# First loads in small pieces on one queue, low parts ahead of squares, and a memory sum placed later in a decoder step's projections

## The chip, the cores and the metric

The kernel runs on one core of a Trainium2 chip. The metric is device microseconds of one execution; the kernel before took 626.89 us (median of 3 runs, 626.23 to 627.23).

## The reference, cut to what matters

One layer of a hybrid decoder is computed for 256 prompt tokens and 32 decode tokens (8 sequences of 4), 288 tokens in all, with model width 2048:

```
mkv  = rms_norm(mem_prompt, mem_norm_g) @ w_mem_kv          # 256 memory tokens -> 8 tiles of 128 columns (4 K, 4 V)
h    = rms_norm(x, norm_g)
z    = h @ w_in                                             # 52 tiles of 128 columns: q, memory q, K/V, convolution, gates
...                                                         # gated convolution, sparse attention, memory attention
y    = x + concat(groups * gates) @ w_out                   # 16 tiles of 128 columns
out  = rms_norm(y, final_g)
```

Two norms matter here: the memory's, whose sum of squares over 2048 entries gives one factor per memory token (`rstd_m`), and x's (`rstd_x`). The outputs are the normed result, all new K and V rows, the memory's K and V, and the updated window and convolution buffers.

## The kernel before, in words

**Layout.** Everything is held transposed: the width of 2048 lies as 16 chunks (k = 0 to 15) of 128 partitions, the tokens lie along the free axis. A weight tile of 128 output columns is 16 blocks of 128x128, loaded as two halves of 128x1024 (512 KB each). Halves are numbered in the order of use, s = 0, 1, 2, ...: s 0 to 15 are the memory's 8 tiles, from s = 16 on come the 52 tiles of the input projection, then the output projection.

**Products.** Halves 0 to 3 (the memory's tiles 0 and 1, `first_tiles`, L267) are multiplied in plain fp32 against the scaled memory; TensorE runs such a matmul as two instructions, so that they are 64. Their order is tile 0, tile 1 for chunks 0 to 7, then tile 0, tile 1 for chunks 8 to 15. From s = 4 on a product is split: a weight's high part (`w_hi`, L221, a rounding copy on ScalarE) and its low part (`w_lo`, L226, raw minus high on VectorE) meet the high and low parts of the activation in three matmuls for each of the half's 8 chunks, 24 in all (`product_half`, L243). In half s ScalarE's copy for half s+2 and VectorE's subtraction for half s+1 are issued first; from half 6 on the low weights are used by the last 8 of the 24 matmuls. Raw halves have 5 buffers, high parts 3, low parts 2. The load of half s+5 or s+6 is issued inside half s, when its buffer's reader has been issued (`w_load`, L214), and it goes on GpSimd's queue from half 5 on, on SyncE's below.

**The order of the work** is written out by hand. `chunk()` (L158) counts a step about every 12 matmuls and lets every running generator issue its next few instructions. A generator's `yield n` means "again n steps later", and `until(VEC)` (L143) means "when a planner's clock for TensorE has passed its clock for VectorE". Every engine then works through its instructions in this order; nothing is reordered on the chip. The step numbers of the start: half 0 ends at step 2, half 1 at 4, half 2 (with tile 0 handed on) at 6, half 3 at 8, half 4 at 10, half 5 at 12, half 6 at 14, half 7 at 16.

**Memory.** 16 chunks of 256 tokens come in pieces (`m_load`, L756); the norm's weights lie in front of chunk 0. `m_scale` (L804) multiplies four chunks by the norm's weights on VectorE, rounds them to the high part on ScalarE and squares the raw values on ScalarE, in place. After halves 1 and 3 VectorE subtracts the low parts (L285). `mem_rstd` (L838) runs from step 7: three additions of 128x1024 on VectorE, two folds, then four tiny matmuls (`ssq`) that sum over partitions, placed at step 10; the factor is computed and spread over partitions by four more matmuls at step 14. Tiles 0 and 1 leave PSUM unscaled and are scaled in SBUF afterwards; tiles 2 to 7 are multiplied by the factor straight out of PSUM (`mem_tile`, L976).

**x.** Its tokens come once as rows (five loads, `xn_load`, L816) for the squares that ScalarE sums at steps 7 to 11 (`sum_x`, L910), and once transposed (`x_load`, L762; four loads of 3, 9, 3 and 1 chunks). `x_load` of the first three chunks is issued in half 2, the others behind the memory's factor (L879), into buffers that hold the memory's raw chunks before. At step 16 x's factor is spread by TensorE, and from step 18 on `prep_x` (L890) scales, rounds and subtracts, three chunks at a time. Its last act, one step after its last subtraction, is `branch_gates` (L945): 32 narrow matmuls of scaled x.

**Around it.** From step 19 on six buffers are filled with cache pages on SyncE's queue (`load_next`, L711), whose products run beside the projections from s = 16 on. Before the first data, WARM = 5 matmuls of zeros keep TensorE busy (L792).

Of the kernel before, what the change touches and what calls it, by code (L numbers as in the profile page):

```python
# [19 lines left out]
KT = 16  # L20
# [43 lines left out]
XSQ_AT = (7, 8, 9, 10, 11)  # L64
X_AT = (16, 17)
KV_ORDER = (2, 4, 3, 5, 0, 1)
# [3 lines left out]
WARM = 5  # L70
# [6 lines left out]
def decode_step(ctx, tc, xT, xN, xD, memT, cst, w_in, w_mem, w_out, w_bg, pt, ptv, ckc, ckk, ckv, wk, wv, mk, mv,  # L77
# [136 lines left out]
    def w_load(s):  # L214
        if s < NH:
            raws[s] = pw.tile([128, 1024], F32, name=f"w{s}", tag="wr", bufs=WR)
            if s > 1:
                (nc.gpsimd if s >= WR else nc.sync).dma_start(raws[s], wsrc[s])  # L218
            loading(DMA_PIECE)
# [23 lines left out]
    def product_half(out, hi, lo, first, last):  # L243
# [10 lines left out]
        for n, (_, a, b) in enumerate(mm):  # L254
            if s == DIRECT and n == 0:
                w_load(s + WR)
            if n == LOAD_AT:
                w_load(s + WR + 1)
            matmul(out, a, b, start=(first and n == 0), stop=(last and n == 23))
# [7 lines left out]
    def first_tiles():  # L267
# [3 lines left out]
        for k0 in (0, 8):  # L271
            for i in range(2):
# [472 lines left out]
    for i in range(3):  # L745
        t = pbig.tile([128, CS if i == 0 else 1024], F32, name=f"mraw{i}", tag="S" if i == 0 else "big", bufs=1 if i == 0 else 3)
        o = KT if i == 0 else 0
        if i == 0:
            mng = t[:, 0:KT]
            m_first = t[:, 0:KT + 512]  # L750
# [5 lines left out]
    def m_load(k, eng=nc.sync):  # L756
        if k == 0:
            eng.dma_start(m_first, memT[:, 0:KT + 512])
        else:
            eng.dma_start(m_raw[k // 4][:, k % 4:k % 4 + 2, :], memT[:, KT + k * 256:KT + (k + 2) * 256].rearrange("p (k n) -> p k n", n=256))  # L760

    def x_load(k0, n):  # L762
# [4 lines left out]
        nc.sync.dma_start(raw[:, :n * NT].rearrange("p (c n) -> p c n", n=NT), xT[:, k0:k0 + n, :])  # L767
        xr.extend(raw[:, j * NT:(j + 1) * NT] for j in range(n))
        xg.extend((k0 + j, raw[:, j * NT:min(j + 3, n) * NT]) for j in range(0, n, 3))
# [31 lines left out]
    macc = m_raw[0].rearrange("p k n -> p (k n)")  # L801
    m_flat = lambda k: m_raw[k // 4].rearrange("p k n -> p (k n)")

    def m_scale(k):  # L804
# [3 lines left out]
        act.activation(m_flat(k), m_flat(k), AF.Square)  # L808

    m_scale(0)  # L810
    m_scale(4)
# [14 lines left out]
    def first_loads(s):  # L826
        if s == 0:
            xn_load(4)
            xn_load(0)
# [759 lines left out]
```

## Time and profile before

| | |
|---|---|
| median of 3 runs | 626.89 us |
| profiled execution | 623.95 us |
| its span, first to last instruction | 621.6 us |
| mean granted TensorE clock | 0.989 |
| HBM read and written | 182.31 MB and 13.60 MB |

How to read it: PE is TensorE's matmuls, PEld its weight loads, DVE is VectorE, ACT ScalarE, POOL GpSimd, SP SyncE. A row of the timeline gives start, length, engine, line, operation, output<-input, shape and count, and in brackets the idle time before it and what ended it. Line L117 is the helper through which all matmuls go, L134 the one for VectorE and ScalarE, so that groups are told apart by their tiles: `zf` is the product of halves 0 to 3, `z` of all others, `mraw` the memory's raw chunks and their squares, `m` its high and low parts, `w`, `wh`, `wl` the weights and their parts, `st` the six buffers (x's rows at first), `rx` x's chunks, `x` its parts, `ssq` the memory's sum and its spread, `Vc` its spread factor, `mixed` (at the start) the scaled memory and the memory's K tiles.

### The profile page before, as it was taken

The page shows a single profiled execution, that of the slowest core. Times are in us where ns is not written, and L with a number is a line of the kernel's source. Part 1 is how long each engine was busy: PE and PEld are TensorE (multiplying, and loading weights), DVE is VectorE, ACT ScalarE, POOL GpSimd, SP SyncE. Part 2 cuts the span into 40 slices and gives each one's busy share as a digit, 9 for nine tenths or more (in the row PEclk, how much of TensorE's full clock was granted, in tenths as well). Part 3 has the DMA queues.
Part 4 walks back from the last instruction along what each step waited for, and adds up shares of the span by engine and source line. Part 5 has one row for each costly group of instructions (what it writes and reads, how often), then busy time and mean ns, then how long its engine had stood idle before and what let it go on. Part 6 is the DMA issues. An engine that isn't in the chain of part 4 may idle for free.

```text
span 621.6 us, 13341 instructions
## 1 busy us (share of the span) xinstructions
PE 605.4 (97%) x4897; PEld 561.1 (90%) x4897; DVE 458.4 (74%) x737; ACT 285.4 (46%) x498; POOL 210.4 (34%) x291
## 2 busy tenths in 40 slices
PE   8899999999999999999999999999999999999993
PEld 6799999989999999988988988988889889999993
DVE  4759899979586689978876879969586533457764
ACT  4736545453555435325334443444534444446560
POOL 2212654535144333324555432323113444122200
PEclk9899999999999999999999999999999999999997
DMA  8999699989989998988888799898979988478723
GB/s 310 396 389 355 218 316 309 354 287 361 330 264 346 390 403 302 372 283 298 285 324 266 243 377 297 307 338 289 388 261 331 331 322 314 143 242 304 234 91 152
DMA packets 74353, 188.40 MB, mean 303 GB/s; under 512 B 8688, under 2 KB 25488, under 8 KB 73904
## 3 DMA queue, kind: packets, MB, share of 16 engines
q0 software_dynamic: 27344, 105.20, 48.0%
q1 hardware_dynamic: 45792, 79.86, 36.2%
q10 hardware_dynamic: 1152, 2.50, 1.2%
q8 instruction: 38, 0.62, 0.4%
q14 instruction: 27, 0.22, 0.1%
HBM read 182.31 MB, written 13.60 MB: 315 GB/s over the span
## 4 chain that ended last, share of the span: by engine, by line
PE 87%; DVE 7%; DMA 2%; issue 2%; ACT 1%; ACTq 0%; DVEq 0%; SPq 0%
PE z L117 70%; PE od L117 3%; PE sk L117 3%; PE acc L117 2%; PE s L117 2%; DVE pooled L134 2%; DMA mraw<-memT 1%; DVE wl L134 1%; PE pt L122 1%; PE pv L122 1%; DVE ysum L134 1%; DVE mraw L134 1%; DMA st<-ckk 1%; DVE st L134 1%; PE smd L117 1%
## 5 line engine op out<-in xcount | busy, mean ns | idle before, releaser
L117 PE MATMUL z<-x,wh 128*128 128x288 f32 x1664 | 255.2, 302 | 0.4 <-ACT wh L134 0.4
L134 DVE TENSOR_TENSOR wl<-w,wh 128x1024 fp32r<-128x1024 f32 x148 | 184.5, 1247 | 81.9 <-PE z L117 47.6
L117 PEld LDWEIGHTS z<-x,wh 128*128 128x128 f32 x1664 | 230.0, 188 | 9.4 <-issue 7.3
L134 ACT ACTIVATE wh<-w 128x1024 fp32r<-128x1024 f32 x148 | 155.0, 1052 | 21.1 <-PE z L117 19.8
L117 PE MATMUL z<-x,wl 128*128 128x288 f32 x832 | 127.1, 295 | 0.1
L117 PEld LDWEIGHTS z<-x,wl 128*128 128x128 f32 x832 | 115.7, 188 | 0.4 <-DVE wl L134 0.4
L344 POOL TENSOR_TENSOR st<-st,cst 128x512 f32<-128x512 f32 x56 | 64.8, 1160 | 115.9 <-issue 57.7
L218 POOL DMA_DIRECT2D w<-w_in x104 | 58.1, 559 | 92.4 <-DVE wl L134 70.9
L134 DVE TENSOR_REDUCE pooled<-st 128x16 f32<-128x1024 f32 x56 | 67.8, 1211 | 10.3 <-POOL st L344 10.3
L134 DVE TENSOR_TENSOR st<-st,cst 128x512 f32<-128x512 f32 x56 | 40.0, 716 | 2.7 <-DMA st<-ckc 2.6
L566 POOL DMA_INDIRECT st<-ckv,rows_v x29 | 30.9, 1066 | 29.1 <-PE od L117 13.9
L218 POOL DMA_DIRECT2D w<-w_out x32 | 17.5, 550 | 59.3 <-DVE wl L134 41.9
L117 PE MATMUL z<-y,wh 128*128 128x288 f32 x256 | 37.0, 297 | 0.0
L117 PE MATMUL z<-y1a,wh 128*128 128x288 f32 x224 | 35.2, 298 | 0.0
L117 PEld LDWEIGHTS z<-y,wh 128*128 128x128 f32 x256 | 35.1, 188 | 0.0
L117 PEld LDWEIGHTS z<-y1a,wh 128*128 128x128 f32 x224 | 31.5, 188 | 1.6 <-issue 0.8
L117 PE MATMUL z<-m,wh 128*128 128x256 f32 x192 | 29.1, 299 | 0.0
L117 PEld LDWEIGHTS z<-m,wh 128*128 128x128 f32 x192 | 26.4, 202 | 0.6 <-issue 0.5
L134 ACT ACTIVATE P<-P,nm 128x128 f32<-128x128 f32 (+1 forms) x32 | 14.2, 444 | 26.7 <-DVE nm L134 26.7
L134 ACT ACTIVATE ysum<-z 128x288 f32<-128x288 f32 x16 | 6.6, 412 | 34.0 <-PE z L117 34.0
L134 ACT ACTIVATE se<-z 128x288 f32<-128x288 f32 x16 | 6.5, 408 | 28.6 <-PE z L117 28.6
L117 PE MATMUL z<-y,wl 128*128 128x288 f32 x128 | 19.6, 296 | 0.0
(283 smaller groups left out, 719.6 us busy)
## 6 DMA issues: line engine op xcount, KB each, us to landing
w<-w_in POOLq DMA_DIRECT2D x104, 512.0 KB, 6.2
st<-ckc SPq DMA_DIRECT2D x112, 256.0 KB, 5.6
w<-w_out POOLq DMA_DIRECT2D x32, 512.0 KB, 4.9
st<-ckk SPq DMA_DIRECT2D x112, 128.0 KB, 4.7
w<-w_mem POOLq DMA_DIRECT2D x11, 512.0 KB, 8.1
o_wk<-wk POOLq DMA_DIRECT2D x8, 512.0 KB, 6.1
o_wv<-wv POOLq DMA_DIRECT2D x8, 512.0 KB, 6.5
qk<-ckc SPq DMA_DIRECT2D x16, 256.0 KB, 6.2
```

The costliest lines, as they stand in the source:

```text
L117: nc.tensor.matmul(out, a, b, **kw)
L122: nc.tensor.transpose(out, a, b)
L134: return getattr(self.engine, name)(*args, **kw)
L218: (nc.gpsimd if s >= WR else nc.sync).dma_start(raws[s], wsrc[s])
L344: done.append(eng.tensor_tensor(tm[:, :, kv], tm[:, :, kv], acmp[:, kv].unsqueeze(1).unsqueeze(1).to_broadcast([128, 2, 4, 64]), op=ALU.mu ...
L566: nc.gpsimd.indirect_dma_start(t, None, ckv, bass.IndirectOffsetOnAxis(ap=rows_v[:, j * 4 + b:j * 4 + b + 1], axis=0))
```

## The change

- **First loads.** Chunk 0 of the memory and chunk 1 come as loads of their own, half 0 comes in pieces of 256, 256 and 512 columns. Half 1 moves from ScalarE's queue to SyncE's. Halves 5 to 13 move from GpSimd's queue to SyncE's (ON_SYNC = 14).
- **x.** Its row pieces are issued one or two with each of halves 0 to 3, behind that half's weight load, and squared at steps 7, 8, 10, 12, 13. Its transposed chunks come in six loads of at most three chunks, one in half 3 and one in each half after it.
- **Memory.** The squares no longer stand in `m_scale`. In half 1 all low parts are issued, and then the first addition, weight 4's high part, and only then the squares of chunks 8 to 15. The running sum has a buffer of its own (`buffers[5]`). `mem_rstd` starts one step later, does two additions and the folds, and places the four `ssq` matmuls at step 13 and the spread at step 17.
- **Tiles 2 and 3** leave PSUM unscaled, as tiles 0 and 1, and are scaled in SBUF.
- WARM is 3 instead of 5, and `branch_gates` starts with `until(VEC)`.

```diff
-XSQ_AT = (7, 8, 9, 10, 11)
+XSQ_AT = (7, 8, 10, 12, 13)
+ON_SYNC = 14
-WARM = 5
+WARM = 3
...
-                (nc.gpsimd if s >= WR else nc.sync).dma_start(raws[s], wsrc[s])
+                (nc.gpsimd if s >= ON_SYNC else nc.sync).dma_start(raws[s], wsrc[s])
...
             if n == LOAD_AT:
                 w_load(s + WR + 1)
+                next(x_next, None)
...
-                        if i == 1:
-                            for k in (k0, k0 + 4):
-                                vec.tensor_tensor(m_hl[1][:, k:k + 4, :], m_g(k, 4), m_hl[0][:, k:k + 4, :].bitcast(F32),
-                                                        op=ALU.subtract)
-                            if k0 == 0:
-                                for k in (8, 12):
-                                    m_scale(k)
+                        if s == 1:
+                            for k in (0, 4):
+                                m_low(k)
+                            for k in (8, 12):
+                                m_scale(k)
+                            for k in (8, 12):
+                                m_low(k)
+                            m_add(4)
+                            w_hi(4)
+                            for k in (8, 12):
+                                m_square(k)
...
+            nc.sync.dma_start(t.rearrange("p (c n) -> p c n", n=NT), xT[:, k0 + j:k0 + j + m, :])
...
+            yield
+    def x_loads():
+        for k0, n in ((0, 3), (3, 9), (12, 3), (15, 1)):
+            yield from x_load(k0, n)
...
-    m_load(0, nc.scalar)
-    nc.sync.dma_start(raws[0][:, :512], wsrc[0][:, :512])
-    m_load(2, nc.scalar)
+    nc.scalar.dma_start(m_first, memT[:, 0:KT + 256])
+    nc.sync.dma_start(raws[0][:, :256], wsrc[0][:, :256])
+    m_load(1, 1, nc.scalar)
+    nc.sync.dma_start(raws[0][:, 256:512], wsrc[0][:, 256:512])
+    m_load(2, 2, nc.scalar)
     nc.sync.dma_start(raws[0][:, 512:], wsrc[0][:, 512:])
-    m_load(4, nc.scalar)
+    m_load(4, 2, nc.scalar)
     m_load(6)
-    nc.scalar.dma_start(raws[1], wsrc[1])
+    nc.sync.dma_start(raws[1], wsrc[1])
...
-    macc = m_raw[0].rearrange("p k n -> p (k n)")
+    macc = buffers[5]
...
+    def m_square(k):
+        act.activation(m_flat(k) if k else macc, m_flat(k), AF.Square)
...
     def mem_rstd():
-        for k in (4, 8, 12):
-            vec.tensor_tensor(macc, macc, m_flat(k), op=ALU.add)
-            yield 1
+        m_add(8)
+        yield 1
+        m_add(12)
+        yield 1
         for n in (512, 256):
             vec.tensor_tensor(macc[:, :n], macc[:, :n], macc[:, n:2 * n], op=ALU.add)
+        yield 3
...
-            if i < 2:
+            if i < 4:
                 vec.tensor_tensor(dst, dst, rstd_m, op=ALU.mult)
...
-        for s, l in ((3, 9), (12, 3), (15, 1)):
-            x_load(s, l)
...
     def branch_gates():
-        yield 1
+        yield from until(VEC)
...
-        if i < 2:
+        if i < 4:
             act.activation(dst, z, AF.Copy)
...
-    spawn(mem_rstd(), 7)
+    spawn(mem_rstd(), 8)
```

More of the change, by code (lines that the diff above doesn't have):

```diff
@@ L748, in decode_step @@
         if i == 0:
-            mng = t[:, 0:KT]
-            m_first = t[:, 0:KT + 512]
+            mng, m_first = t[:, 0:KT], t[:, 0:KT + 256]
         m_raw += [t[:, o + j * 1024:o + (j + 1) * 1024].rearrange("p (k n) -> p k n", n=256) for j in range(2 if i == 0 else 1)]
@@ L754, in decode_step, with m_load @@
     xr, xg = [], []
[L756 to L760, printed above, removed]
+    def m_load(k, n=2, eng=nc.sync):
+        eng.dma_start(m_raw[k // 4][:, k % 4:k % 4 + n, :], memT[:, KT + k * 256:KT + (k + n) * 256].rearrange("p (k n) -> p k n", n=256))
     def x_load(k0, n):
@@ L766, in x_load @@
             raw = pbig.tile([128, 1024], F32, name=f"rx{k0}", tag="big")
-        nc.sync.dma_start(raw[:, :n * NT].rearrange("p (c n) -> p c n", n=NT), xT[:, k0:k0 + n, :])
-        xr.extend(raw[:, j * NT:(j + 1) * NT] for j in range(n))
-        xg.extend((k0 + j, raw[:, j * NT:min(j + 3, n) * NT]) for j in range(0, n, 3))
+        for j in range(0, n, 3):
+            m = min(3, n - j)
+            t = raw[:, j * NT:(j + m) * NT]
+            nc.sync.dma_start(t.rearrange("p (c n) -> p c n", n=NT), xT[:, k0 + j:k0 + j + m, :])
+            xr.extend(t[:, i * NT:(i + 1) * NT] for i in range(m))
+            xg.append((k0 + j, t))
+            yield
+    def x_loads():
+        for k0, n in ((0, 3), (3, 9), (12, 3), (15, 1)):
+            yield from x_load(k0, n)
+    x_next = x_loads()
     w_load(0)
     w_load(1)
-    m_load(0, nc.scalar)
-    nc.sync.dma_start(raws[0][:, :512], wsrc[0][:, :512])
-    m_load(2, nc.scalar)
+    nc.scalar.dma_start(m_first, memT[:, 0:KT + 256])
[3 more added lines that the diff above has]
+    m_load(2, 2, nc.scalar)
     nc.sync.dma_start(raws[0][:, 512:], wsrc[0][:, 512:])
-    m_load(4, nc.scalar)
+    m_load(4, 2, nc.scalar)
     m_load(6)
-    nc.scalar.dma_start(raws[1], wsrc[1])
+    nc.sync.dma_start(raws[1], wsrc[1])
     m_load(8)
@@ L807, in m_scale, with m_low, m_add @@
         act.activation(m_hl[0][:, k:k + 4, :], m_g(k, 4), AF.Copy)
-        act.activation(m_flat(k), m_flat(k), AF.Square)
-    m_scale(0)
-    m_scale(4)
+    def m_low(k):
+        vec.tensor_tensor(m_hl[1][:, k:k + 4, :], m_g(k, 4), m_hl[0][:, k:k + 4, :].bitcast(F32), op=ALU.subtract)
+    def m_square(k):
+        act.activation(m_flat(k) if k else macc, m_flat(k), AF.Square)
+    def m_add(k):
+        vec.tensor_tensor(macc, macc, m_flat(k), op=ALU.add)
+    for k in (0, 4):
+        m_scale(k)
+        m_square(k)
     sums = small(6, "xsum", 1)
@@ L829, in first_loads @@
             xn_load(0)
+        elif s == 1:
             xn_load(1)
-        elif s == 1:
-            xn_load(2)
-            xn_load(3)
             nc.gpsimd.tensor_scalar(rows_v, rows_v, 32.0, C("row"), op0=ALU.mult, op1=ALU.add)
         elif s == 2:
-            x_load(0, 3)
+            xn_load(2)
+        elif s == 3:
+            xn_load(3)
+            next(x_next)
     def mem_rstd():
-        for k in (4, 8, 12):
-            vec.tensor_tensor(macc, macc, m_flat(k), op=ALU.add)
-            yield 1
+        m_add(8)
+        yield 1
+        m_add(12)
+        yield 1
         for n in (512, 256):
             vec.tensor_tensor(macc[:, :n], macc[:, :n], macc[:, n:2 * n], op=ALU.add)
+        yield 3
         yield from token_rstd(rstd_m, [macc[:, 0:256]], 256, 1)
@@ L977, in mem_tile @@
         dst = mkT[:, i, :] if i < 4 else zt("A", "mvt")[:, :256]
-        if i < 2:
+        if i < 4:
             act.activation(dst, z, AF.Copy)
         else:
-            yield 3 if i == 2 else 2
+            yield 2
             assert "rstd_m" in env
```

## The prediction

> **What bounds the kernel now.** I read the profile page first (its busy shares and the chain that ended last), then who waited for whom on TensorE, then TensorE's timeline from the start, then VectorE's timeline and the granted clock in the one stretch where TensorE stood still.
>
> ```profile
> span 621.6 us, 13341 instructions
> ...
> PE 605.4 (97%) x4897; PEld 561.1 (90%) x4897; DVE 458.4 (74%) x737; ACT 285.4 (46%) x498; POOL 210.4 (34%) x291
> ...
> PE 87%; DVE 7%; DMA 2%; issue 2%; ACT 1%; ACTq 0%; DVEq 0%; SPq 0%
> ```
>
> TensorE is busy for 97% of the span and carries 87% of the chain, so what the change can win is only time in which TensorE stands still or runs slowly. The longest wait on it is one single wait:
>
> ```profile
> PE ssq L117 <- DVE mraw L134: 3.1, 1, 3.1
> ```
>
> It is the four matmuls that sum the memory's squares over partitions. They stand in TensorE's order behind half 4, and VectorE has not folded the squares yet. TensorE's timeline around it:
>
> ```profile
> 1.15 5.17 PE L117 MATMUL zeros<-zeros 128*128 128x288 f32 x10 [1.15 <-POOL zeros L789]
> 6.52 2.37 PE L117 MATMUL zf<-mixed,w 128*128 128x256 f32 x8 [0.20 <-DVE mixed L134]
> 9.61 12.36 PE L117 MATMUL zf<-mixed,w 128*128 128x256 f32 x56 [0.72 <-DVE mixed L134]
> ...
> 24.18 0.64 PE L117 MATMUL z<-m,wl 128*128 128x256 f32 x4
> 27.93 1.01 PE L117 MATMUL ssq<-cst,mraw 128*128 128x1 f32 x4 [3.10 <-DVE mraw L134]
> 28.80 2.91 PE L117 MATMUL z<-m,wh 128*128 128x256 f32 x12
> ...
> 34.30 2.17 PE L117 MATMUL z<-m,wh 128*128 128x256 f32 x16
> ...
> 41.44 2.17 PE L117 MATMUL z<-m,wh 128*128 128x256 f32 x16
> ...
> 44.41 2.08 PE L117 MATMUL z<-m,wh 128*128 128x256 f32 x16
> ...
> 47.28 2.08 PE L117 MATMUL z<-m,wh 128*128 128x256 f32 x16
> ```
>
> Half 4 ends at 24.18 + 0.64 = 24.82, half 5 starts at 28.80 and half 6 only at 34.30. An undisturbed half takes 47.28 - 44.41 = 2.87 us. Half 5 therefore took 5.50 us instead of 2.87, and the granted clock says why (windows of 2 us; TensorE's share of full speed is the last figure but two, then DMA's share and GB/s):
>
> ```profile
> 26.00:28.00 2.00, 0.07 (x1) 0.07 (x1) 1.93 (x4) 1.09 (x3) 0.38 (x1) 0.80 1.04 409
> ...
> 32.00:34.00 2.00, 2.00 (x11) 1.97 (x10) 0.00 (x0) 0.00 (x0) 0.00 (x0) 0.50 0.96 401
> 34.00:36.00 2.00, 2.00 (x18) 1.84 (x17) 1.30 (x7) 1.25 (x2) 0.00 (x0) 0.99 0.97 334
> ```
>
> The stall put the clock at half (0.80 means that it fell at about 27.2) and it stayed there to about 34.0. So one wait of 3.10 us costs 34.30 - 24.82 = 9.48 us for work that needs one half and a few small matmuls.
>
> **The change part by part.** *The memory's sum.* VectorE's order before the sum:
>
> ```profile
> 20.93 2.35 DVE L134 TENSOR_TENSOR m<-mixed,m 128x1024 fp32r<-128x1024 f32 x2
> 23.20 1.22 DVE L134 TENSOR_TENSOR mraw<-mraw,mraw 128x1024 f32<-128x1024 f32 x1
> 24.33 1.22 DVE L134 TENSOR_TENSOR wl<-w,wh 128x1024 fp32r<-128x1024 f32 x1
> 25.47 1.22 DVE L134 TENSOR_TENSOR mraw<-mraw,mraw 128x1024 f32<-128x1024 f32 x1
> 26.72 1.15 DVE L134 TENSOR_TENSOR mraw<-mraw 128x512 f32<-128x512 f32 x2
> ```
>
> VectorE works here without a break and ends the folds at 27.87. The change takes two things out of this stretch: the low parts of k = 8 to 15 (2.35 us, now right behind their high parts, ahead of half 4) and the first addition (1.22, now behind them). By that alone the folds end near 27.87 - 2.35 - 1.14 = 24.4. Then the sum's matmuls move from the end of half 4 to the middle of half 6, that is to about 24.8 + 2.87 + 1.43 = 29.1. That leaves a margin of 4.7 us, so I cost this wait at nothing; if ScalarE's last square came 4.7 us later, the wait would be back. Without the gap the clock has no reason to fall. What remains of that stretch is one half (2.87) and the sum's four matmuls, 28.80 - 27.93 = 0.87 at half rate and so 0.44 at full, with 0.2 for two tiny ones for x's sums, wherever they now stand: 3.5 us against 9.48. **Gain 6.0 us.** What could be late next is half 6's low weights: VectorE makes them once half 4 frees their buffer, at 24.8 + 1.22 = 26.0, and half 6, from 27.7, asks for them after 16 of its 24 matmuls, at 29.6.
>
> [...]
>
> *First loads.* TensorE's unbroken run starts at 9.61, when the fifth chunk of the memory has landed:
>
> ```profile
> 9.20 1.14 DVE L134 TENSOR_SCALAR mixed<-mraw 128x256 f32<-128x256 f32 x4 [1.23 <-DMA mraw<-memT]
> ```
>
> How much was moved by then (windows as above):
>
> ```profile
> 2.00:4.00 2.00, 2.00 (x5) 1.43 (x5) 0.00 (x0) 1.34 (x2) 1.63 (x4) 1.00 0.83 168
> 4.00:6.00 2.00, 2.00 (x5) 1.06 (x4) 0.00 (x0) 0.14 (x1) 0.00 (x0) 1.00 0.91 319
> 6.00:8.00 2.00, 1.77 (x6) 1.00 (x6) 1.24 (x4) 0.00 (x0) 0.00 (x0) 1.00 1.07 406
> 8.00:10.00 2.00, 1.28 (x6) 0.81 (x6) 0.80 (x4) 2.00 (x2) 0.00 (x0) 1.00 1.04 399
> 10.00:58.00 48.00, 44.90 (x306) 42.94 (x305) 36.87 (x67) 27.74 (x41) 9.62 (x18) 0.93 1.02 397
> 58.00:80.00 22.00, 22.00 (x190) 20.73 (x190) 19.18 (x27) 11.91 (x21) 11.11 (x14) 1.00 0.69 220
> ```
>
> On ScalarE's queue 776 KB stand up to that chunk before (264 + 256 + 256) and after (136 + 128 + 256 + 256), and SyncE's queue shares the engines with 768 KB in both. Halving the first pieces lets chunk 0 start some tenths earlier (from 6.52), but chunk 4 decides: all 1,544 KB of both queues (1.58 MB) are moved by 7.5 us at the windows' rates (0.34 + 0.64 MB by 6.0, then 406 GB/s), while the chunk landed at 9.2. So it comes at most 1.7 us earlier and about not at all later; nearest is the same byte count at the same place in its queue, and I take 0.3 earlier. Against that stand two fewer warm-up matmuls: 10 instructions took 5.17 us there, 0.52 each, where full rate gives 12.36 / 56 = 0.22 for 256 columns, so the array starts at half rate (the clock column reads 1.00 in these windows; the pace does not). Six instructions end near 4.3, the array then idles until the first chunk, and full rate may come some tenths after 9.6. Taken: 0.3 lost. **Start 0, ends +1.7 and -2.2** (the lower one below).
>
> *One queue.* Weights 5 to 13 leave GpSimd's queue for SyncE's, between x's rows and pieces. Each waits there for its buffer, and what is queued behind it waits too: 5 to 8 for the ends of halves 0 to 3, 9 to 13 for low parts of VectorE. DMA runs at 397 GB/s from 10 to 58, so the order of bytes sets the landing. Up to weight 7 stand the memory (2.1 MB), weights 0 to 7 (4.2), early constants (0.1) and three row pieces of x (1.3), 7.7 MB; weight 8 and two more row pieces make 9.3. With 1.8 MB moved by 8.0 these are through at 22.9 and 26.9 us, and land at most 1.7 later (9.2 against 7.5 above). Weight 7 is first used in half 7, near 31, and needs 1.1 us of ScalarE before. Cost nothing; the cover is the 5 us of prefetch, and each us beyond it would be paid in full. Splitting x's load into six pieces adds two issues on SyncE, off the path.
>
> *Tiles 2 and 3, x's preparation.* Two ScalarE copies replace two PSUM multiplications, which become SBUF ones. The memory's factor now comes in half 8, just ahead of x's scaling on VectorE:
>
> ```profile
> 37.26 0.61 PE L117 MATMUL ssq<-cst,yr 128*128 128x128 f32 x4
> 37.91 0.39 ACT L134 ACTIVATE Vc<-ssq 128x256 f32<-128x256 f32 x1 [2.07 <-PE ssq L117]
> ...
> 42.30 1.37 DVE L134 SCALAR_TENSOR_TENSOR rx<-rx,cst,rstd_x 128x288 f32<-128x288 f32 x3
> ...
> 58.90 1.23 DVE L134 TENSOR_TENSOR wl<-w,wh 128x1024 fp32r<-128x1024 f32 x1
> ...
> 61.16 1.12 PE L117 MATMUL z<-m,wl 128*128 128x256 f32 x8
> ```
>
> VectorE's groups from 37 to 64.4 (count, busy us, mean ns, idle before):
>
> ```profile
> L134 DVE TENSOR_TENSOR wl<-w,wh 128x1024 fp32r<-128x1024 f32 x9 | 11.0, 1224 | 1.3 <-ACT x L134 1.0 <-issue 0.3
> ...
> L134 DVE TENSOR_TENSOR mixed<-mixed,Vc 128x256 f32<-128x256 f32 x2 | 0.8, 422 | 1.5 <-ACT Vc L134 1.5
> ```
>
> Before, scaling starts 42.30 - 41.44 = 0.86 us into half 8. After, VectorE must wait there for 12 matmuls (1.43), the spread (0.61), the copy (0.39) and do two multiplications (0.8 for both at most): 3.1 to 3.2 us in. Of these 2.3 us more, 1.0 was idle before anyway and the spread's 0.6 delays TensorE as well; the two further multiplications add 0.7. VectorE so runs 1.4 us later against TensorE through halves 9 to 14, where its work per half exceeds a half. The tightest place is half 14: its low weights are ready at 60.13 and used at 61.16, slack 1.03. **Cost 0.4 us**, ends 0 and 1.5. The gates' 32 matmuls are only moved, behind the last scaling instead of one step after it, and ScalarE's squares only stand behind weight 4's high part; I cost both at nothing, since VectorE's next use of the gates has halves of time and the squares have the 4.7 us margin above.
>
> *Sum:* 6.0 + 0 - 0.4 = 5.6. The profiled execution took 623.95 us (2.35 around its span of 621.6), so 618.35 with a span of 616.0. The median of the three runs, 626.89, lies 2.94 above the profiled execution; the same distance kept, 621.3. From half 16 on TensorE is fed as before, some 6 us earlier; DMA's share of 0.69 from 58 to 80 is the room for that.
>
> **The rivals.** *A cold start.* The half rate after the stall lasted from the restart at 27.93 to 34.0, 6.1 us of work. If the three warm-up matmuls do not count and such a stretch begins with the first chunk, some tenths before 6.52, say 5.7, it ends at 11.8, and 2.2 us at half rate past the 9.6 of the unbroken run lose 1.1; one stretch of pieces with gaps in between may double it. Gain 3.4 to 4.5, time 622.4 to 623.5. For it: the work comes in dribbles up to 9.2. Against: eight matmuls before 9.6 did not hinder full rate now. [...]
>
> *VectorE takes over.* If it runs 3 us later in halves 9 to 14 instead of 1.4, TensorE waits 2 us there, and a gap of that kind may touch the clock: gain 1 to 3.5, time 623.4 to 625.9. For: the busy stretch without idle. Against: it is 1 us short only at its end.
>
> *Slower: x's factor comes late.* The row pieces of x (each 512 KB, and the median us from issue to landing) are squared by ScalarE, in order, ahead of x's factor and of weight 9's high part.
>
> ```profile
> st<-xN SPq DMA_DIRECT2D x4, 512.0 KB, 11.8
> ```
>
> ScalarE's group of these squares from 6 to 32, and the first and last steps of the factor on VectorE:
>
> ```profile
> L134 ACT ACTIVATE st<-st 128x1024 f32<-128x1024 f32 x4 | 4.2, 1048 | 0.0
> ```
>
> ```profile
> 34.40 0.15 DVE L134 COPY xs<-rx 32x1 f32<-32x1 f32 x1 [3.86 <-PE rx L117]
> ...
> 35.52 0.16 DVE L134 SCALAR_TENSOR_TENSOR yr<-yt,yr 128x3 f32<-128x3 f32 x1
> ```
>
> The last piece is now issued behind half 3's end, near 22. With the 11.8 us that such a piece took before, it lands at 33.8, its square (1.05) and the factor (1.28) end at 36.1, and TensorE, which wants the factor at the start of half 8 near 34.0, waits 2.1 us. From a wait of about 3 us the clock falls too, which costs 2.6 more as in half 5: at a landing from 34.7 on the gain of 5.6 is gone, and each us later is lost at once, 627 to 630. Against: by the bytes above it lands before 28.6, and the factor is then ready in time.
>
> *It does not do it.* The sum still waits (a square on ScalarE behind a late load): 626 to 627.
>
> **How the numbers follow.** Forecast 0.60; cold start 0.17; VectorE 0.10; slower 0.08; not done 0.05. A measurement of this kernel tells about 0.2% (1.25 us) from no change. Faster: the first three less a remainder, 0.86; same 0.06; slower 0.08. The range's low end is the start's and VectorE's better ends together (5.6 + 1.7 + 0.4, so 619.2) less the 0.7 by which the lowest of the three runs lies under their median: 618.5. Its high end holds the cold start and most of VectorE's case: 625.2. It leaves out "not done" and the slower case.
>
> **What would show it.** In the changed profile: no TensorE wait on the sum; granted clock 1.00 from about 10 on; half 6 begins near 28 and half 8 near 35; a short wait at most on the low weights of half 14; the first projection of x about 6 us earlier than before. Wrong: a gap of over 2 us on TensorE before 65, a clock of 0.50 past 12, or a later stage that gives the 6 us back, so that the end moves by less than half 16 does.

## The result, and the profile after

| | before | after |
|---|---|---|
| median of nine executions each | 623.96 us (622.92 to 627.23) | 618.64 us (618.22 to 622.86) |
| ratio | | 0.9922, 95% interval 0.9892 to 0.9951 |
| profiled execution, its span | 623.95, 621.6 us | 622.86, 620.4 us |
| mean granted clock | 0.989 | 0.994 |

The change is 5.3 us faster by the medians. Two things must be kept in mind with these numbers. The three times of before that were shown first (626.23 to 627.23) were the slowest of its nine. And the profiled execution of after is the slowest of its nine; the spans of five others are 616.5 to 616.7. So the trace of after shows the gain at the start whole, and at the end only a part of it.

From the page of after (span; busy time of the engines; the chain that ended last):

```profile
span 620.4 us, 13332 instructions
...
PE 601.8 (97%) x4893; PEld 557.0 (90%) x4893; DVE 458.0 (74%) x737; ACT 286.3 (46%) x500; POOL 203.5 (33%) x282
...
PE 77%; DVE 10%; DMA 8%; issue 2%; ACT 1%; SPq 0%; ACTq 0%; DVEq 0%
```

TensorE still carries the chain, but VectorE and DMA have taken 10 and 8% of it, against 7 and 2% before. Who waited for whom on TensorE (total, times, longest):

```profile
PE sk L118 <- DMA st<-ckk: 2.5, 2, 1.7
...
PE acc L118 <- DVE pcT L135: 0.7, 1, 0.7
...
PE z L118 <- DVE mvt L135: 0.5, 1, 0.5
PE pt L123 <- DVE P L135: 0.5, 1, 0.5
```

The wait on the memory's sum is gone from this list. In its place stand several shorter ones, most of them late in the kernel. TensorE's timeline at the start of after:

```profile
1.15 3.25 PE L118 MATMUL zeros<-zeros 128*128 128x288 f32 x6 [1.15 <-POOL zeros L803]
4.45 1.80 PE L118 MATMUL zf<-mixed,w 128*128 128x256 f32 x4
6.95 1.13 PE L118 MATMUL zf<-mixed,w 128*128 128x256 f32 x4 [0.69 <-DVE mixed L135]
9.03 12.35 PE L118 MATMUL zf<-mixed,w 128*128 128x256 f32 x56 [0.95 <-DVE mixed L135]
...
23.61 0.64 PE L118 MATMUL z<-m,wl 128*128 128x256 f32 x4
...
26.97 1.60 PE L118 MATMUL z<-m,wh 128*128 128x256 f32 x12
28.41 0.50 PE L118 MATMUL ssq<-cst,st 128*128 128x1 f32 x4
...
34.37 1.69 PE L118 MATMUL z<-m,wh 128*128 128x256 f32 x12
...
40.64 2.08 PE L118 MATMUL z<-m,wh 128*128 128x256 f32 x16
...
53.08 1.66 PE L118 MATMUL z<-m,wh 128*128 128x256 f32 x12 [0.50 <-DVE mvt L135]
...
61.27 1.88 PE L118 MATMUL z<-x,wh 128*128 128x288 f32 x12
```

Half 4 ends at 24.25 and half 6 begins at 26.97, 2.72 us later instead of 9.48; the sum's four matmuls follow at 28.41 inside half 6, with no wait. The granted clock there (same columns as in the prediction's windows):

```profile
28.00:30.00 2.00, 2.00 (x19) 2.00 (x19) 0.45 (x1) 2.00 (x4) 0.00 (x0) 1.00 1.03 409
...
32.00:34.00 2.00, 2.00 (x18) 1.91 (x17) 1.73 (x6) 1.48 (x3) 0.00 (x0) 1.00 1.06 417
```

It stays at 1.00, in every window from 26 to 38. VectorE in after: the folds, the memory's factor arriving, x's scaling, and the last multiplication straight out of PSUM ahead of half 14:

```profile
24.21 1.15 DVE L135 TENSOR_TENSOR st<-st 128x512 f32<-128x512 f32 x2
...
36.95 0.76 DVE L135 TENSOR_TENSOR mixed<-mixed,Vc 128x256 f32<-128x256 f32 x2 [1.65 <-ACT Vc L135]
37.63 1.37 DVE L135 SCALAR_TENSOR_TENSOR rx<-rx,cst,rstd_x 128x288 f32<-128x288 f32 x3
...
52.52 0.41 DVE L135 TENSOR_TENSOR mvt<-z,Vc 128x256 f32<-128x256 f32 x1
```

In what follows, the *lead* of a kernel at a half is how much earlier that half starts in its profile than in that of before (half 4 at 21.61, half 10 at 47.28, half 16 at 67.26), and the lead at the end is the difference of the spans. After's lead is 0.57 at half 4, 6.64 at half 10, 5.99 at half 16, 6.41 at half 38. Then half 43 takes 11.85 us instead of the 8.18 it takes in before, and two waits on cache keys stand in it:

```profile
158.26 0.59 PE L118 MATMUL sk<-st,qz 128*32 128x256 f32 x2 [0.76 <-DMA st<-ckk]
...
160.55 1.02 PE L118 MATMUL sk<-st,qz 128*32 128x256 f32 x10 [1.70 <-DMA st<-ckk]
```

At half 44 it is 2.50, at half 62 it is 2.66, at half 110 it is 1.44 and at the end 1.2 us.

### The profile page after: what moved, and what is told of

It is laid out like the page before. It is cut to its first block, busy times and chain, and to the rows that moved or that the text cites. A ratio compares the mean times of both kernels' runs of the same rounds, so it can differ in the third digit from the quotient of the medians.

```text
span 620.4 us, 13332 instructions
## 1 busy us (share of the span) xinstructions
PE 601.8 (97%) x4893; PEld 557.0 (90%) x4893; DVE 458.0 (74%) x737; ACT 286.3 (46%) x500; POOL 203.5 (33%) x282
## 3 DMA queue, kind: packets, MB, share of 16 engines
q10 hardware_dynamic: 1152, 1.97, 0.8%
## 4 chain that ended last, share of the span: by engine, by line
PE 77%; DVE 10%; DMA 8%; issue 2%; ACT 1%; SPq 0%; ACTq 0%; DVEq 0%
PE z L118 59%; PE od L118 3%; DMA st<-ckk 3%; PE sk L118 3%; DMA st<-ckc 3%; DVE pooled L135 2%; PE zf L118 2%; DVE wl L135 2%; PE acc L118 2%; DMA rx<-xT 2%; PE s L118 2%; DMA mraw<-memT 1%; DVE st L135 1%; PE pt L123 1%; DVE ysum L135 1%
## 5 line engine op out<-in xcount | busy, mean ns | idle before, releaser
L350 POOL TENSOR_TENSOR st<-st,cst 128x512 f32<-128x512 f32 x56 | 62.8, 1121 | 132.9 <-issue 68.2
L118 PE MATMUL z<-m,wh 128*128 128x256 f32 x192 | 27.3, 287 | 0.5 <-DVE mvt L135 0.5
L118 PEld LDWEIGHTS z<-m,wh 128*128 128x128 f32 x192 | 24.7, 191 | 0.8 <-issue 0.7
L118 PE MATMUL sk<-st,qz 128*32 128x256 f32 x288 | 20.5, 382 | 2.5 <-DMA st<-ckk 2.5
```

Of the source, the lines that this page charges most:

```text
L118: nc.tensor.matmul(out, a, b, **kw)
L350: done.append(eng.tensor_tensor(tm[:, :, kv], tm[:, :, kv], acmp[:, kv].unsqueeze(1).unsqueeze(1).to_broadcast([128, 2, 4, 64]), op=ALU.mu ...
```

## The experiments

Each was timed on one chip together with runs of the kernel before; "profile" is one execution of each.

| kernel | ratio to before, 95% interval | start of half 4 | lead at half 16 | lead at the end |
|---|---|---|---|---|
| after | 0.9922 (0.9892 to 0.9951) | 21.04 | 5.99 | 1.2 |
| e1: the sum's part alone | 0.9959 (0.9940 to 0.9978) | 21.79 | 3.87 | 2.4 |
| e2: all but the sum's part | 1.0016 (0.9998 to 1.0034) | 20.72 | 1.97 | -3.5 |
| e3: before, gap filled | 0.9978 (0.9954 to 1.0003) | 21.78 | 2.53 | 1.5 |
| e4: after, sum at step 10 | 0.9947 (0.9927 to 0.9968) | 20.91 | 5.39 | 2.9 |
| after once more | 0.9923 (0.9903 to 0.9944) | 23.71 | 3.29 | 2.3 |
| e5, e9: after, WARM = 5 | 0.9905 (0.9885 to 0.9925), 0.9912 (0.9880 to 0.9944) | 20.86, 20.76 | 6.14, 6.25 | 5.2, 3.5 |
| e10: after, WARM = 1 | 0.9917 (0.9884 to 0.9950) | 21.77 | 5.32 | 2.9 |
| e6: after, GpSimd's queue | 0.9907 (0.9888 to 0.9926) | 21.88 | 4.50 | 3.9 |
| e7: after, gates early | 0.9964 (0.9938 to 0.9990) | 21.58 | 5.33 | 0.6 |
| e11: before, gates late | 1.0015 (0.9994 to 1.0036) | 21.89 | -0.28 | -1.9 |
| e8: after, WARM = 5, all copies | 0.9991 (0.9970 to 1.0012) | 20.92 | 3.95 | -0.3 |

**e1: the memory's sum alone.** Before, with the new order of low parts, additions and squares, the sum at step 13, and tiles 2 and 3 scaled in SBUF.

```diff
-                        if i == 1:
+                        if s == 1:
...
+                            m_add(4)
+                            w_hi(4)
...
+        yield 3
         yield from token_rstd(rstd_m, [macc[:, 0:256]], 256, 1)
...
-    spawn(mem_rstd(), 7)
+    spawn(mem_rstd(), 8)
```

> The kernel before with the memory's part alone: low parts and first addition in half 1, squares behind them, the sum's matmuls at step 13, tiles 2 and 3 scaled in SBUF; all loads, queues and the five warm-up matmuls as before. If the wait and the half clock behind it carry the gain: no TensorE wait on the sum, full clock throughout, half 6 begins near 27.7 to 28.5, the first product of x near 61.5 to 62 (before 67.26, after 61.27), time 5 us under before. If the small loads and the one queue carry it: the first product of x stays above 65 and the time is within 1.5 us of before.

Measured: 621.87 us against 625.06, 3.2 us and not 5. TensorE's timeline of this kernel:

```profile
29.50 0.50 PE L117 MATMUL ssq<-cst,st 128*128 128x1 f32 x4
...
47.99 1.68 PE L117 MATMUL z<-m,wh 128*128 128x256 f32 x12 [0.50 <-DVE mvt L134]
...
55.10 1.66 PE L117 MATMUL z<-m,wh 128*128 128x256 f32 x12 [0.50 <-DVE mvt L134]
```

No wait on the sum, and the lead is 5.89 at half 10. By half 16 it has lost 2.0 of that, after only 0.65: VectorE is late (0.50 us twice on `mvt`, beside smaller waits), for it starts to scale x 39.65 - 35.12 = 4.5 us into its half 8, and in after 37.63 - 34.37 = 3.3 us in. VectorE's row in e1:

```profile
39.65 1.37 DVE L134 SCALAR_TENSOR_TENSOR rx<-rx,cst,rstd_x 128x288 f32<-128x288 f32 x3
```

What makes VectorE late stands in ScalarE's timeline of e1:

```profile
37.61 1.06 ACT L134 ACTIVATE wh<-w 128x1024 fp32r<-128x1024 f32 x1 [1.97 <-DMA w<-w_mem]
38.58 0.37 ACT L134 ACTIVATE Vc<-ssq 128x256 f32<-128x256 f32 x1
```

The copy of the memory's factor comes behind the high part of half 10, for whose weight ScalarE waits. In after that high part starts at 34.78 without a wait and the copy at 36.54. Up to 70 us ScalarE waits 6.6 us for weights in e1 and 1.5 us in after.

So the sum's part removes the wait and the fall of the clock (half 5's first 12 matmuls take 1.60 us here and 2.91 in before; the mean clock is 0.995 against 0.989), and the other part helps it to keep what it won: 63.40 - 61.27 = 2.1 us at half 16, of which 0.75 lie in the start of half 4. Which of the loads does the rest was not tried, apart from the queue (e6).

**e2: everything else alone.** After, with the memory's low parts, squares, additions and sum back where they were, and tiles 2 and 3 multiplied out of PSUM.

```diff
-                        if s == 1:
+                        if i == 1:
...
-    spawn(mem_rstd(), 8)
+    spawn(mem_rstd(), 7)
```

> The changed kernel with the memory's part undone: small first loads, one queue, x in six pieces and three warm-up matmuls stay, but low parts, squares, additions, the sum's matmuls (step 10) and tiles 2 and 3 stand as before. If the wait and the clock carry the gain: a TensorE wait of about 3 us on the sum, clock 0.50 behind it, the first product of x near 66 to 67, time 0 to 1 us under before. If loads and queue carry it: first product of x under 64, time 3 to 5 us under before.

Measured: 625.35 us against 625.06, no gain that can be told. In this kernel's timeline the wait is there again, and in its windows the fall of the clock:

```profile
27.26 0.61 PE L118 MATMUL ssq<-cst,st 128*128 128x1 f32 x4 [3.33 <-DVE st L135]
```

```profile
28.00:30.00 2.00, 2.00 (x14) 2.00 (x14) 0.96 (x6) 1.20 (x3) 0.00 (x0) 0.67 1.01 402
30.00:32.00 2.00, 2.00 (x11) 2.00 (x11) 0.00 (x0) 0.38 (x1) 0.00 (x0) 0.50 1.04 420
32.00:34.00 2.00, 2.00 (x19) 2.00 (x18) 1.23 (x1) 1.72 (x3) 0.00 (x0) 0.98 1.04 408
```

The half rate lasts 1.32 + 2.00 + 0.08 = 3.4 us here and 0.80 + 6.00 + 0.04 = 6.8 us in before, by the same windows (0.50 in all three from 28 to 34). The lead of 1.97 at half 16 is made of 0.89 by which half 4 starts earlier and of 1.7 from a slow stretch that is 3.4 us shorter at half rate, less 0.2 for the longer wait and some lag behind it. The first product of x came at 65.29, a little earlier than expected. The kernel gives it all back later (lead -3.5 at the end).

**e3: the gap filled.** Before, with 26 matmuls that nobody reads on TensorE ahead of the sum. The extra work is no part of the reference.

```diff
+        for _ in range(26):
+            nc.tensor.matmul(ps[:, 128:384], m_hl[0][:, 0, 0:128], m_hl[0][:, 0, :], start=True, stop=True)
         for k, p in enumerate(planes):
```

> The kernel before with 26 more matmuls of the memory's high part in front of the sum's four (their result is overwritten by nothing that is read); they fill the 3.1 us in which TensorE waited and change nothing else. If the fall of the clock is half of the loss: clock 1.00 through 26 to 36, half 5 takes about 2.9 us instead of 5.5, the first product of x near 64.6, time 2.6 us under before. If the clock does not matter or falls anyhow: the first product of x at 67 or later, time equal to before or up to 0.5 us over.

Measured: 623.08 us against 625.06; the interval of the ratio reaches 1.0003, so the time alone doesn't quite show a gain. Its timeline:

```profile
24.83 3.28 PE L872 MATMUL ssq<-m 128*128 128x256 f32 x26
28.09 0.60 PE L117 MATMUL ssq<-cst,mraw 128*128 128x1 f32 x4
```

The sum's matmuls stand no earlier than before, but half 5's first 12 matmuls behind them take 1.68 us and not 2.91, the mean clock is 0.996 against 0.989, and the lead at half 16 is 2.53. In this profile that is the price of the clock alone: of the 6 us that one wait costs, about 2.5 us are half rate and 3.5 us are the wait itself with what stands around it.

**e4: the sum's matmuls back at step 10.** After, without the three steps ahead of the sum.

```diff
-        yield 3
-        yield from token_rstd(rstd_m, [macc[:, 0:256]], 256, 1)
+        yield from token_rstd(rstd_m, [macc[:, 0:256]], 256, 4)
```

> The changed kernel with the sum's four matmuls back at step 10, behind half 4; everything else, the spread at step 17 too, as changed. The folds end near 25.3 there and half 4 near 24.1. If moving the low parts ahead did most of it and the place is only margin: a TensorE wait of about 1.2 us, clock 1.00, the first product of x near 62.4, time 1.2 us over the changed kernel (4 under before). If the place is what counts: a wait of 2.5 us or more, the clock falls, the first product of x near 66.

Measured: 621.21 us against 625.06. The wait is shorter than I had expected:

```profile
24.46 0.61 PE L118 MATMUL ssq<-cst,st 128*128 128x1 f32 x4 [0.33 <-DVE st L135]
```

Half 5's first 12 matmuls behind it take 1.68 us (2.91 in before), the mean clock is 0.994, and the lead at half 10 is 6.04 against after's 6.64. So nearly all of the gain comes from VectorE folding earlier; the later place of the matmuls adds 0.3 to 0.7 us (0.33 is the wait; between halves 4 and 10 this kernel gains 5.34 us and after 6.07) and a margin.

**After once more.** No edit.

> The changed kernel unchanged, beside its variants on one chip. Its first profile gave 5.99 us at the first product of x and kept 1.2 of it at the span's end; TensorE waited there 2.5, 2.0 and 1.7 us on loads of cache keys between halves 38 and 44, which the kernel with the sum at step 10 did not do. If these waits belong to single executions (theory A), this profile shows the first product of x at 61.1 to 61.5 us, waits on st<-ckk of under 1 us together, and a span of 616 to 618. If they belong to the order of this kernel (theory B), they are there again, over 4 us in all, and the span is near 620. Time: 0.990 to 0.994 of the kernel before in both.

Measured: 620.22 us (618.48 to 621.68) against 624.88. The expectation misread the row of these waits in after's first profile: 2.5, 2, 1.7 is a total of 2.5 us in two waits, the longer 1.7. Theory A of the waits on cache keys holds: none is over 0.3 us here, so they belong to single executions. The first product of x was missed, though, and with it the span (619.3): it came at 63.98, because this execution started cold. Its timeline:

```profile
5.01 2.07 PE L118 MATMUL zf<-mixed,w 128*128 128x256 f32 x4 [0.61 <-DVE mixed L135]
7.79 15.41 PE L118 MATMUL zf<-mixed,w 128*128 128x256 f32 x56 [0.71 <-DVE mixed L135]
```

The same 56 instructions took 12.35 us in after's first profile. Taken one by one, they start 0.43 us apart up to 13.9 and 0.22 apart behind that. The granted clock doesn't show it; a window of this kernel (clock: last figure but two) counts four matmuls in one us at a clock of 1.00:

```profile
10.00:11.00 1.00, 1.00 (x4) 0.73 (x3) 0.82 (x1) 1.00 (x3) 0.00 (x0) 1.00 1.04 401
```

This is the rival called "a cold start", in one execution of the very kernel; it costs 23.71 - 21.04 = 2.7 us at half 4, and the lead is still 2.7 us shorter than in after's first profile at half 38, ahead of the waits on cache keys.

**e5 and e9: five warm-up matmuls.**

```diff
-WARM = 3
+WARM = 5
```

> The changed kernel with five warm-up matmuls instead of three. The forecast put the whole start at nothing, with 0.3 us lost to the shorter warm-up. Ten instructions of zeros took 4.82 to 5.17 us and six took 3.25. Theory A, the two matmuls only stand in the way of the first chunk: its products then start near 6.0 us and not at 4.45, but the unbroken run of 56 still starts near 9.0, behind the fifth chunk, and the first product of x lies within 0.3 us of the unchanged variant; time within 0.2%. Theory B, the longer warm-up raises the clock sooner: the first matmuls of the memory take 0.22 us each and not 0.45, the unbroken run ends earlier by 0.3 to 0.6, time up to 0.1% shorter. Theory C, they delay the run: it starts 0.3 to 0.8 us later and so does everything behind it.

> The changed kernel with five warm-up matmuls, once more. With three, half 4 began at 20.72 to 21.04 us in three profiles and at 21.58, 21.88 and 23.71 in three others, whose first products ran at 0.43 us each, half pace, until 10.5 to 14.0 us; with five it was at 20.86 and at full pace from 4.7. Theory A, five are enough for the clock to rise before the first product, three only in some executions: half 4 starts at 20.7 to 21.1 again, and the executions scatter by less than those of the changed kernel (618.2 to 622.9 in nine, 618.5 to 621.7 in six), with the median at 0.988 to 0.992 of the kernel before. Theory B, the rise falls at random and the first profile was luck: half 4 later than 21.5, scatter as with three.

Measured: 618.35 us (618.27 to 620.05) against 624.88, and 620.22 (619.93 to 621.08) against 625.26. The start of e5:

```profile
1.15 4.50 PE L118 MATMUL zeros<-zeros 128*128 128x288 f32 x10 [1.15 <-POOL zeros L803]
...
8.86 12.35 PE L118 MATMUL zf<-mixed,w 128*128 128x256 f32 x56 [0.78 <-DVE mixed L135]
```

By the distances between matmuls full pace began at 4.7 us in e5, at 4.2 in e9 (the ten warm-up instructions took 4.50 and 4.25 us there, 5.17 in before), and at 7.1 or earlier in all seven profiles with WARM = 5 (the others are before, e1, e3, e8 and e11). Of the six with WARM = 3 it was there by 7.6 in three (after, e2, e4) and for good only at 10.5 to 14.0 in the other three (e6, e7, after once more). In the time this doesn't show: the two medians with five, 618.35 and 620.22, are much like those of after in its two comparisons, 618.64 and 620.22. So theory A of e5 holds in time and in the first product of x (61.12, and 61.27 in after's first profile), though its first matmuls ran at full pace, as theory B had it. In e9 the figures of theory A came (half 4 at 20.76, a scatter of 1.2 us, 0.9912); but e6, with three warm-ups, scatters by 1.2 us as well, so the scatter doesn't tell the two apart. With three warm-ups full pace began anywhere from 5.0 to 14.0 us, and why isn't shown.

**e10: one warm-up matmul.**

```diff
-WARM = 3
+WARM = 1
```

> The changed kernel with one warm-up matmul, two instructions, instead of three matmuls. Theory A, the array needs an unbroken stretch of work before its clock rises, and the pieces of the memory with their gaps up to 9.0 us do not count as one: the first products run at 0.43 us each until 11 to 14 us in every execution, half 4 starts at 22 to 24 us, and the time is 1 to 2.7 us (0.2 to 0.4%) above that with five. Theory B, the warm-up hardly matters, because the rise falls at random: half 4 between 20.7 and 21.9, time as with three.

Measured: 620.64 us against 625.26, level with e9 on the same chip. Its start:

```profile
5.33 5.84 PE L118 MATMUL zf<-mixed,w 128*128 128x256 f32 x16 [2.85 <-DVE mixed L135]
11.35 10.63 PE L118 MATMUL zf<-mixed,w 128*128 128x256 f32 x48 [0.19 <-DMA w<-w_mem]
```

Full pace came at about 8.7 us and half 4 at 21.77, 1.0 later than in e9. Theory A is not borne out: full pace came ahead of 11 us, and the time is 0.4 us above e9's. Theory B's figures came, half 4 between 20.7 and 21.9 and the time as with three; that the rise falls at random is more than this one profile can show.

**e6: weights 5 to 13 back on GpSimd's queue.**

```diff
-ON_SYNC = 14
+ON_SYNC = 5
```

> The changed kernel with halves 5 to 13 back on GpSimd's queue. The forecast cost the one queue at nothing. Theory A: order on the queue does not matter, because 5 us of prefetch cover it: no TensorE wait on a weight's load either way, the last row piece of x lands within 3 us of 28.5, the first product of x within 0.5 us of the unchanged variant, time within 0.2%. Theory B: the two queues share the engines, so weights of later halves take bandwidth from x's row pieces; these then land 2 us or more later, x's factor and its spread move behind the start of half 8 and TensorE waits there 1 us or more; time 0.2 to 0.5% longer. Theory C: the single queue itself holds pieces back behind a weight that waits for its buffer; with two queues x's pieces land 2 us or more earlier, without effect on TensorE.

Measured: 619.49 us against 624.88, level with after (620.22) and e5 (618.35) on the same chip. The last row piece of x is issued at 13.64 and lands at 27.58; in after it is issued at 20.33 and lands at 28.52. TensorE waits for no weight's load in either. TensorE waited 0.35 us on x's factor in e6, and the first product of x lay 1.5 us behind that of after's first profile, 0.84 of it from a start that was cold until 10.8; so theory A's 0.5 us was missed. The rest, 0.65 us, is lost behind half 6: half 7's weight lands at 27.77 in e6 and at 24.68 in after, ScalarE waits 2.20 us for it, and x's squares and factor stand behind it. In the time theory A holds: within what can be told here, the queue is worth nothing. In this start the granted clock does show the slow stretch:

```profile
8.00:9.00 1.00, 1.00 (x4) 0.34 (x2) 0.41 (x2) 1.00 (x2) 0.00 (x0) 0.50 0.89 277
```

The matmuls from 4.52 to 7.20 had run at full pace already (0.32 us from the first to the second, 0.58 in after once more), so here the pace was lost again while the first loads came in pieces.

**e7: the gates early again.** This was to win back what after loses late.

```diff
     def branch_gates():
-        yield from until(VEC)
+        yield 1
```

> The changed kernel with the gates' 32 matmuls back one step after x's last scaling. In all three kernels with the gates' later start, small products downstream (gates, selection, cache keys, attention) stand half a half to two halves later in TensorE's order than in the kernel before, and between halves 62 and 110 these kernels lost about 2 us on waits for VectorE (pcT 0.7 to 1.4, P 0.5 to 0.9), which the kernel with the memory's sum alone did not. Theory A, the shifted order costs them: here the small products stand where they stood before, the waits are gone, the lead at the end is the lead at half 16 less under 1.5 us, and the time is 1.5 to 2.5 us (0.25 to 0.4%) shorter than that of the unchanged variant. Theory B, the order does not matter and the waits come from TensorE running earlier against VectorE and the loads: time within 0.2% of the unchanged variant. Theory C, slower: VectorE is still busy with x when the gates are asked for, and TensorE waits for it in half 15, over 0.5 us.

Measured: 623.13 us (619.63 to 627.27) against 624.88, and 2.9 us *slower* by the medians than the unchanged variant beside it; the two intervals overlap by a little (0.9938 to 0.9944). Theory A of this experiment falls, on the wrong side. There is no wait in half 15 either, so C falls too: the lead at half 16 is 5.33. It is lost far behind. Rows from 355 on of e7's timeline:

```profile
359.02 0.47 PE L118 MATMUL acc<-pcT,vcp 96*128 96x512 f32 x1 [1.79 <-DVE pcT L135]
...
404.28 1.02 PE L118 MATMUL sk<-st,qz 128*32 128x256 f32 x10 [1.57 <-DMA st<-ckk]
```

The small products stand where they stood in before, and, as I read it, there is no room there for a kernel that is 4 to 5 us ahead: half 89 takes 6.74 us instead of 5.41 in before, half 99 takes 7.79 instead of 5.25. In e1, which has the same order and a lead of 3.8, half 99 takes 6.71. In eight profiles with the later order (after twice, e2, e4, e5, e6, e9, e10) the product with the cache keys of half 99 comes half a half later, and TensorE doesn't wait there for cache keys. The product at the end of half 89 stands at the same place in both orders, so its wait of 1.79 us is not explained by this, and e1 does not have it.

**e11: the gates late, alone.**

```diff
     def branch_gates():
-        yield 1
+        yield from until(VEC)
```

> The kernel before with one edit of the change alone: the gates' products wait for the planner. That moves the 32 gate matmuls by half a half and the small products downstream by half a half to two halves. Taking this edit out of the changed kernel made it 2.9 us slower by the medians on one chip: in its profile TensorE waited 1.57 us on cache keys between halves 99 and 100 and 1.79 us on VectorE in half 90, against 0.45 in half 90 and no wait on cache keys before. Theory A, the later order by itself is worth 2 to 4 us, because it gives the cache loads and VectorE more room whatever the lead: 0.994 to 0.997 of the kernel before, and the first product of x within 0.3 us of before. Theory B, the order is worth something only for a kernel with a lead of 4 us or more, since without a lead the loads are there in time: within 0.2% of the kernel before, with 1.1 to 1.2 us lost between halves 62 and 110 as in the changed kernel. Theory C, in the kernel before the later order only costs: 1 us or 0.2% slower.

Measured: 625.00 us against 624.43. From its waits on TensorE:

```profile
PE pt L122 <- DVE P L134: 0.9, 1, 0.9
PE acc L117 <- DVE pcT L134: 0.7, 1, 0.7
```

Theory B: in a kernel without a lead the later order wins nothing. In the profile it costs 1.7 us between halves 62 and 110; in the time no cost can be told (0.9994 to 1.0036). Together the four make a table of two by two: early order without and with the lead 1 and 0.9964, late order 1.0015 and 0.9922. By this table the order pays only with the lead.

**e8: no multiplication out of PSUM.** Five warm-ups, and tiles 4 to 7 copied by ScalarE as well.

```diff
-WARM = 3
+WARM = 5
...
-            if i < 4:
-                vec.tensor_tensor(dst, dst, rstd_m, op=ALU.mult)
+            vec.tensor_tensor(dst, dst, rstd_m, op=ALU.mult)
...
-        if i < 4:
-            act.activation(dst, z, AF.Copy)
-        else:
-            yield 2
-            assert "rstd_m" in env
-            vec.tensor_tensor(dst, z, rstd_m, op=ALU.mult)
+        act.activation(dst, z, AF.Copy)
         mem_raw[i] = dst
+        yield 1
```

> The changed kernel with five warm-up matmuls, and with the memory's tiles 4 to 7 copied out of PSUM by ScalarE as well and scaled in SBUF afterwards. In half 14 TensorE waited 0.50 us for mvt, the tile that VectorE multiplies straight out of PSUM. Theory A, the wait is for the bank that this multiplication frees: it is gone here, nothing takes its place, and the first product of x starts 0.4 to 0.6 us ahead of the variant with five warm-ups (61.1). Theory B, the wait is VectorE's lag as the forecast had it, and shows at the next product that needs VectorE, the low weights of half 14: TensorE waits 0.3 to 0.6 us there. Time: 0.4 to 0.6 us less than with five warm-ups in A and equal in B, if the order of the small products behind half 16 stays; if the copies shift that order, the lead at the end may differ by up to 4 us either way, as with the earlier gates.

Measured: 624.92 us against 625.26; the lead is 6.76 at half 10 and 3.95 at half 16. Its timeline:

```profile
52.96 1.22 PE L118 MATMUL z<-m,wl 128*128 128x256 f32 x8 [1.19 <-DVE wl L135]
...
56.35 1.22 PE L118 MATMUL z<-m,wl 128*128 128x256 f32 x8 [0.26 <-DVE wl L135]
...
60.09 1.22 PE L118 MATMUL z<-m,wl 128*128 128x256 f32 x8 [0.38 <-DVE wl L135]
```

Theory B, and more than it asked for: the wait on `mvt` is gone, and 1.8 us on the low weights of halves 13, 14 and 15 stand in its place. VectorE is what is short in halves 9 to 15 (in after it works without a break from 36.95 to 61.15); the bank was only where it showed. Why these waits add up to more than the 0.50 us on `mvt` in after isn't shown. Behind half 16 the small products moved again, by up to four halves, and the rest of the lead went with them (1.51 us on `P` in half 78, 0.86 on cache keys in half 55, and others). Which of the moved products is to blame wasn't tried.

## Why the prediction was right, and where it wasn't

- **The wait and the clock, 6.0 us.** Right in mechanism and size: 6.64 - 0.57 = 6.1 us between halves 4 and 10. e1 shows that the memory's part alone does it (5.89 + 0.18 = 6.1), e3 that the clock is 2.5 of it. The folds end at 25.36 and not at 24.4, since VectorE waited 0.75 us for a high part of ScalarE and had a reduction in between; the margin to 28.41 was 3.05 us instead of 4.7, and enough.
- **The start, 0.** Half 4 came 0.57 us earlier, since the fifth chunk let the unbroken run begin at 9.03 instead of 9.61; inside the ends. What I called a rival beside the forecast, the cold start, isn't one fixed outcome: it takes some executions of the same kernel and spares others. It came in three of six profiles with three warm-ups and in none of seven with five, so the shorter warm-up may let it in; so few profiles don't show it. I priced it at 1.1 to 2.2 us; against after's first profile it cost 0.5, 0.8 and 2.7 us at half 4 in the three that had it.
- **One queue, 0.** Right for the time: TensorE waited for no weight's load in after or e6, and e6 is level. In the profiles the loads are worth something: with two queues half 7's weight lands 3.1 us later and half 16 starts 0.65 us later (e6, less its cold start), and with all the old loads the lead at half 16 is 2.1 us shorter (e1).
- **VectorE's lag, 0.4.** Right in cause and size for the whole change (0.65 us between halves 10 and 16); with the old loads it is 2.0 (e1). Scaling starts 3.26 us into half 8 (3.1 to 3.2 forecast), VectorE then has no break up to half 15, and TensorE waits 0.50 us in half 14. I expected the wait on the low weights; it stood on the PSUM bank that VectorE frees in the same order (the multiplication out of it ends at 52.93, half 14 starts at 53.08). e8 turned it into the other, and with 1.8 us of such waits came near the rival "VectorE takes over", which had priced 2.
- **x's factor late, the slower rival.** Not seen: the last piece landed at 28.52, forecast before 28.6.
- **The sum, 5.6.** Measured 5.3 by the medians here and 4.7 in the second comparison, 5.99 at half 16. That the end comes so near is in part luck: the start gave 0.6 us that was not forecast, and later stages took what was not forecast either. The absolute figure, 621.3, is 2.7 too high because it hung on the three slowest times of before; 618.64 lies only 0.1 above the low end of the range.
- **"From half 16 on TensorE is fed as before."** This is the step that failed, and the forecast's own sign for it, an end that moves by less than half 16 does, came in both profiles of after (1.2 against 5.99, 2.3 against 3.29) and in all its variants. The lead doesn't stay by itself: between halves 62 and 110 after loses 1.2 us in each of its two profiles on waits that its shifted order brings (`pt` 0.48 and `acc` 0.69 us among them), and in the one profile 3.9 us more between halves 38 and 44, 2.5 of them in the two waits on cache keys. The forecast listed the gates as "only moved" and costed that at nothing. In fact the move shifts many of the small products behind it by half a half to a whole one. By itself it costs 1.7 us in that stretch of e11's profile, though none that the time can show; without it 2.9 us of the gain would be lost (e7). That these two come out near the forecast together was not foreseen.

What stays open: why the cache keys of halves 38 to 44 come late in some executions (after's first profile, e2) and not in others with the same order, and whether the scatter of 618.2 to 622.9 us is that or the cold start; both were seen, and each is big enough. For the keys the traces narrow it down: after issues the last three loads for half 43 at 148.50 to 149.82, and they land 9.6 to 10.6 us later. In e5, whose half 43 starts 0.36 us earlier, they are issued at 147.85 to 149.40 and land after 6.2 to 6.3 us. So the transfers took longer; what slowed them isn't shown.

## What to carry to other kernels

Behind the waits of 3.10 us in before and 3.33 us in e2 TensorE's granted clock read 0.50, and e11, with a wait of 3.1 us, has a mean clock of 0.990 beside before's 0.989. Behind after's wait of 1.70 us (to 160.55) and e7's of 1.57 us (to 404.28) it read 1.00, and e7, which had one of 1.79 us as well, has a mean of 0.995 beside after's 0.994. So look at the granted clock behind a wait before pricing it. Here the clock made 2.5 of 6 us. A lead won at the start has to be carried past every later place where loads or another engine are just in time, so compare the starts of the same product all along both traces, not only at the end. An edit that "only moves" a few instructions in front of a planner can move much of what the planner places behind them; price the order, not the instructions.

## What the runs showed of the hardware that I had not expected

- After one gap of about 3 us TensorE ran at half rate (granted clock 0.50) for 6.8 us in before and 3.4 us in e2, though the gap of e2 was the longer one (3.33 against 3.10).
- With the same three warm-up matmuls full pace began anywhere between 5.0 and 14.0 us in six profiles; the granted clock column showed it in one of the three late ones (e6, 0.50 from 8 to 9 us, 0.992 in the mean). It read 1.00 in every window up to 17 us of after once more, and its mean in e7 is 0.995; there only the distance between matmuls showed it (0.43 against 0.22 us).
- Every kernel scattered over 1 to 8 us from one execution to the next on one chip (e7: 619.63 to 627.27), so single profiles can be compared half by half but not by their ends.
